# Differential attention's output, computed with the queries on the partitions, block by block

## The chip, the cores and the metric

The kernel runs on one core of a Trainium2 chip. The metric is device time in microseconds (us) for one execution. A core has a matrix engine (TensorE, PE in the profile, with its weight loads shown as PEld), a vector engine (VectorE, DVE), a scalar engine (ScalarE, ACT), a general one (GpSimd, POOL) and a queue engine (SyncE, SP) that starts transfers. Each engine works through its own instructions in the order in which they stand in its queue and waits on semaphores of the others.

## What is computed

Two transformer blocks, one after the other, on 512 tokens of width 1024. The change is in the second block's differential attention, eight heads of 128 value columns:

```python
# q, k: (B, S, H, 2, 64) after an RMS norm; v: (B, S, H, 128)
s = jnp.einsum("bhmqd,bhmkd->bhmqk", qblk, kt).astype(jnp.float32) * scale
s = s + bias[None, :, None]                    # distance bias of the head
s = jnp.where(dist >= 0, s, -jnp.inf)          # causal
p = jax.nn.softmax(s, axis=-1)
a = (p[:, :, 0] - lam * p[:, :, 1]).astype(vt.dtype)
o = jnp.einsum("bhqk,bhkd->bhqd", a, vt)
...
o = rms_norm_2(o, subln_g) * (1.0 - lambda_init)   # over the head's 128 columns
o = o.reshape(B, S, DIFF_WIDTH) * jax.nn.silu(gate)
return o @ w_proj
```

The block also has a convolution branch (31 taps over 1024 channels, then a layer norm), a cross-attention branch over 256 memory tokens, and a gated sum of the three branches.

## The kernel before, in words

All arithmetic is float32 in effect: an operand is split into a high part (a rounded copy, made by ACT) and a low part (the rest, made by DVE or POOL by a subtraction), and a product takes three matmuls, high by high, high by low, low by high. In the names, `hh`/`hl` are the normed input's two parts, `wh`/`wl` those of a weight block, `pth`/`ptl` those of the transposed attention weights, `dvh`/`dvl` those of the values.

The second block's attention stage runs from about 400 us to about 735 us of the span. `staged` walks over 32 items, eight heads `h` by four query blocks `n` of 128 queries. In step `i` it calls `diff_first` on item `i` (scores, mask and minimum on DVE, exponentials on ACT, then DVE divides and subtracts the two maps), `diff_pv` on item `i-2`, `diff_tp` on item `i-1` (PE transposes the attention weights, ACT and DVE split them), and then `fill`, which issues one to three pieces of other work: projections of the queries, keys, values and gates of later heads and of the other branches, 24 or 12 matmuls each, with their weight loads and splits. The instructions of an engine stand nearly in this order. An exception is the convolution (`cv`, L902 and L904, 31 DVE operations for each of eight channel groups), which has a low priority and is laid between other DVE work when the program is built; the order is fixed from then on.

The steps that the change touches, per head: `causal_tp` fills one pair of tiles `pth`/`ptl` over all four query blocks. At the head's last block, `diff_pv` multiplies them with the values, which are the stationary operand, so that the output lies with the value columns on the partitions and the 512 queries along the row (L1056, twelve matmuls of 512, 384, 256 and 128 columns, three each). ACT squares the output and copies it out of PSUM (L1059, L1060). In the next head's steps, `rsum` sums the squares over the partitions by a product with a column of ones (L225), ten small DVE operations make the reciprocal root (`rsqrt_small`), `rdiag` writes its four blocks as diagonal matrices (L234), `rbc` multiplies them with ones to spread them over the partitions (L240), and DVE scales the output by them and by the gain (L1070). `spill` multiplies by the gate (L933), splits (L934, L935) and stores both parts for the projection that comes later. PSUM tiles come from small pools: two for scores (`sc`), two for transposes and sums (`tp`), one for the attention output (`pv`), three for projections (`mm`).

Of the kernel before, what the change touches and what calls it, by code (L numbers as in the profile page):

```python
# [11 lines left out]
F32 = mybir.dt.float32  # L12
# [8 lines left out]
P = 128  # L21
S = 512
# [71 lines left out]
def two_block_kernel(ctx: ExitStack, tc: tile.TileContext, A: dict, out: bass.AP):  # L94
# [229 lines left out]
    with ExitStack() as st:  # L324
# [119 lines left out]
        after(dve.tensor_scalar(out=sub8, in0=V("subln"), scalar1=0.8, scalar2=None, op0=ALU.mult), first)  # L444
# [426 lines left out]
    with ExitStack() as st:  # L871
        wk = open_pool(st, "wk2", 2, reuse_waits="tile")
        dp = open_pool(st, "dp", 2, reuse_waits="tile")
        cm_[0] = open_pool(st, "cm2", 1, reuse_waits="tile")
# [88 lines left out]
        def dv_gen(g):  # L963
            w = w2("dv", g)
            vh = dp.tile([P, NT, CW], F32R, tag="dvh", name="dvh")
            vl = dp.tile([P, NT, CW], F32R, tag="dvl", name="dvl")
            for tp in range(2):
# [5 lines left out]
                pv_ = ps.rearrange("p (t d) -> p t d", t=2)  # L973
                d = slice(2 * tp, 2 * tp + 2)
                act.copy(out=vh[:, d, :], in_=pv_)
                dve.tensor_tensor(out=vl[:, d, :], in0=pv_, in1=f(vh[:, d, :]), op=ALU.subtract)
                yield
            D["dv", g] = (vh, vl)
# [56 lines left out]
        def diff_tp(it):  # L1035
            h, n = it
            causal_tp(it, D.pop(it), n, (n + 1) * P, ("dpt", h))

        def diff_pv(it):
            h, n = it  # L1040
            if n == 0 and h > 0:
                D["ss", h - 1] = rsum(D.pop(("oq", h - 1)))
            if n == 1 and h > 0:
                D["dg", h - 1] = rdiag(wk, D.pop(("ss", h - 1)), 1.0 / 128, 1e-6, "or")
            if n == 2 and h > 0:
                diff_out(h - 1)
            if n < NT - 1:
                return
            pth, ptl = fxd.pop(("dpt", h))
            vh, vl = D["dv", h // 2]  # L1050
            c0 = (h % 2) * P
            pv = pv_tile()
            for j in range(NT):
                a, b = vh[:, j, c0:c0 + P], vl[:, j, c0:c0 + P]
                for i, (l_, r_) in enumerate(((a, pth), (a, ptl), (b, pth))):
                    pe.matmul(out=pv[:, j * P:], lhsT=l_, rhs=r_[:, j, j * P:], start=(j == 0 and i == 0), stop=(j == NT - 1 and i == 2))  # L1056
            o = wk.tile([P, S], F32, tag="do", name="do", bufs=3)
# [4 lines left out]
            if h == 7:  # L1062
                D["ss", h] = rsum(q)
# [378 lines left out]
```

## Time and profile before

| | us |
|---|---|
| median of 3 runs | 1195.09 |
| lowest, highest | 1194.05, 1196.65 |
| profiled execution, its own time | 1196.61 |
| its span (first to last instruction) | 1194.8 |
| PE busy in the span | 1154.0 (97%) |
| DVE busy in the span | 926.6 (78%) |
| ACT busy in the span | 551.7 (46%) |
| POOL busy in the span | 213.3 (18%) |

A busy share is an average over stages, and a matmul's recorded duration includes time in which the next one has started already. What a matmul costs in a stream is the distance from its start to the start of the next.

### The profile page before, as it was taken

How to read it: one execution, taken by the hardware profiler on the slowest of the kernel's cores; microseconds unless marked ns; L12 is line 12 of the kernel's file. 1: busy time of each engine (PE TensorE's matmuls, PEld its weight loads, DVE VectorE, ACT ScalarE, POOL GpSimd, SP SyncE). 2: the span in 40 equal slices, each digit the busy share in tenths (PEclk: the TensorE clock that was granted, in tenths of full speed). 3: DMA queues.
4: the chain of work that ended last, by engine and by line, in shares of the span. 5: the costliest groups of instructions: out<-in, count | busy, mean ns of one | idle time of the engine just before them, and what ended most of it. 6: DMA issues, size and time to landing. Idle time of an engine off the chain costs nothing.

```text
span 1194.8 us, 18995 instructions
## 1 busy us (share of the span) xinstructions
PE 1154.0 (97%) x6960; PEld 1015.9 (85%) x6960; DVE 926.6 (78%) x2055; ACT 551.7 (46%) x1173; POOL 213.3 (18%) x161
## 2 busy tenths in 40 slices
PE   7879999999989999999999999999999999999998
PEld 6878887878889988998999887988888888888898
DVE  6997777898686699999989999999692596543341
ACT  7646566557554354445554452544422354232230
POOL 1334200000112211120111221221010132011020
PEclk9989999999999999999999999999999999999999
DMA  8765312443463423324233343333446755433232
GB/s 336 259 212 164 105 56 87 152 148 110 150 231 131 124 71 98 106 89 115 89 116 106 124 141 106 106 116 106 152 147 227 267 186 185 132 97 101 86 123 79
DMA packets 61965, 165.43 MB, mean 138 GB/s; under 512 B 7120, under 2 KB 15568, under 8 KB 60848
## 3 DMA queue, kind: packets, MB, share of 16 engines
q1 hardware_dynamic: 36560, 122.41, 32.5%
q10 hardware_dynamic: 25312, 41.82, 10.0%
q8 instruction: 55, 0.90, 0.3%
q14 instruction: 38, 0.31, 0.1%
HBM read 136.80 MB, written 20.58 MB: 132 GB/s over the span
## 4 chain that ended last, share of the span: by engine, by line
PE 63%; DVE 24%; issue 3%; ACT 1%; DMA 0%; POOL 0%; ACTq 0%; DVEq 0%; POOLq 0%
PE mm L190 40%; PE mm L199 15%; DVE cv L904 7%; DVE wl L171 3%; DVE dp L1025 1%; PE pv L773 1%; DVE dp L1032 1%; PE tp L751 1%; DVE dp L1031 1%; DVE ptl L754 1%; PE sc L1157 1%; PE pv L694 1%; PE pv L1200 1%; DVE qs L259 1%; PE tp L266 1%
## 5 line engine op out<-in xcount | busy, mean ns | idle before, releaser
L169 ACT CAST wh<-raw 128x512 fp32r<-128x512 f32 x372 | 215.3, 620 | 217.7 <-PE mm L190 96.2
L171 POOL TENSOR_TENSOR wl<-raw,wh 128x512 fp32r<-128x512 f32 (+1 forms) x93 | 141.8, 1525 | 831.9 <-ACT wh L169 668.8
L171 DVE TENSOR_TENSOR wl<-raw,wh 128x512 fp32r<-128x512 f32 (+1 forms) x279 | 201.7, 747 | 95.3 <-ACT wh L169 94.9
L190 PE MATMUL mm<-hh,wh 128*128 128x512 f32 x640 | 255.9, 400 | 0.0
L190 PE MATMUL mm<-hh,wl 128*128 128x512 f32 x640 | 251.8, 393 | 0.0
L190 PE MATMUL mm<-hl,wh 128*128 128x512 f32 x640 | 251.7, 393 | 0.0
L199 PE MATMUL mm<-wh,hh 128*128 128x256 f32 (+1 forms) x672 | 193.5, 289 | 0.2 <-ACT hh L824 0.2
L904 DVE SCALAR_TENSOR_TENSOR cv<-u,vec,cv 128x512 f32<-128x512 f32 x240 | 191.1, 796 | 3.4
L199 PE MATMUL mm<-wl,hh 128*128 128x256 f32 (+1 forms) x672 | 190.7, 284 | 0.3 <-POOL wl L171 0.3
L199 PE MATMUL mm<-wh,hl 128*128 128x256 f32 (+1 forms) x672 | 190.8, 284 | 0.0
L190 PEld LDWEIGHTS mm<-hh,wl 128*128 128x128 f32 x640 | 120.5, 188 | 27.0
L190 PEld LDWEIGHTS mm<-hh,wh 128*128 128x128 f32 x640 | 120.6, 188 | 24.7
L190 PEld LDWEIGHTS mm<-hl,wh 128*128 128x128 f32 x640 | 120.8, 189 | 24.5
L199 PEld LDWEIGHTS mm<-wl,hh 128*128 128x128 f32 x672 | 128.5, 191 | 0.8 <-POOL wl L171 0.6
L199 PEld LDWEIGHTS mm<-wh,hh 128*128 128x128 f32 x672 | 127.9, 191 | 0.8 <-ACT hh L824 0.5
L199 PEld LDWEIGHTS mm<-wh,hl 128*128 128x128 f32 x672 | 128.3, 191 | 0.0
L190 PE MATMUL mm<-bh,wh 128*128 128x512 f32 x192 | 75.9, 396 | 0.0
L190 PE MATMUL mm<-bh,wl 128*128 128x512 f32 x192 | 75.4, 393 | 0.0
L190 PE MATMUL mm<-bl,wh 128*128 128x512 f32 x192 | 75.4, 393 | 0.0
L1027 ACT ACTIVATE dp<-dp,dst 128x128 f32<-128x128 f32 (+3 forms) x64 | 35.5, 556 | 54.8 <-DVE dst L1025 54.6
L199 PE MATMUL mm<-wl,mh 128*128 128x256 f32 x128 | 39.3, 307 | 6.5 <-DVE wl L171 6.5
L190 PEld LDWEIGHTS mm<-bl,wh 128*128 128x128 f32 x192 | 36.1, 188 | 8.4 <-issue 0.2
(326 smaller groups left out, 2122.4 us busy)
## 6 DMA issues: line engine op xcount, KB each, us to landing
raw<-in_w_dram SPq DMA_DIRECT2D x120, 512.0 KB
raw<-in_w_out_dram SPq DMA_DIRECT2D x24, 512.0 KB
raw<-in_w_mem_dram SPq DMA_DIRECT2D x16, 512.0 KB
ada<-in_w_ada_dram SPq DMA_DIRECT2D x8, 1024.0 KB
ada<-in_w_gate_dram SPq DMA_DIRECT2D x8, 512.0 KB
k<-ks SPq DMA_DIRECT2D x32, 128.0 KB
o_d<-sph ACTq DMA_DIRECT2D x16, 256.0 KB
o_d<-spl ACTq DMA_DIRECT2D x16, 256.0 KB
```

Source lines behind the costliest of these rows:

```text
L169: act.copy(out=wh[:, s], in_=raw[:, s])
L171: eng.tensor_tensor(out=wl[:, s], in0=raw[:, s], in1=f(wh[:, s]), op=ALU.subtract)
L190: m = pe.matmul(out=ps, lhsT=a[:, c0:c0 + P], rhs=at(b, k), start=(n == 0 and i == 0), stop=(n == KT - 1 and i == 2))
L199: pe.matmul(out=ps, lhsT=at(a, k)[:, t * P:(t + 1) * P], rhs=b[:, 0:n], start=(start and m == 0 and i == 0), stop=(stop and m == len(order ...
L259: dve.scalar_tensor_tensor(out=s[b], in0=ps[a], scalar=sc, in1=f(s[a]), op0=ALU.mult, op1=ALU.subtract)
L266: pe.transpose(out=ps[:, t * P:(t + 1) * P], in_=src[:, t, c0:c0 + P], identity=ident)
L694: pe.matmul(out=pv4[0:64], lhsT=l_, rhs=r_[:, j], start=(cnt == 0), stop=(cnt == 3 * nk - 1))
L751: pe.transpose(out=tp[:, j * P:(j + 1) * P], in_=pt_[:, j * P:(j + 1) * P], identity=ident)
L754: dve.tensor_tensor(out=ptl[:, 0:n + 1, n * P:w], in0=tv, in1=f(pth[:, 0:n + 1, n * P:w]), op=ALU.subtract)
L773: pe.matmul(out=pv[0:64, j * P:], lhsT=l_, rhs=r_[:, j, j * P:], start=(j == 0 and i == 0), stop=(j == NT - 1 and i == 2))
L904: dve.scalar_tensor_tensor(out=a, in0=u[:, j:j + S], scalar=dw[:, m * 31 + j:m * 31 + j + 1], in1=a, op0=ALU.mult, op1=ALU.add)
L1027: act.activation(out=p_[:, :w], in_=p_[:, :w], func=AF.Exp, scale=-1.0, bias=st_[:, 0, n, m:m + 1], accum_out=st_[:, 1, n, m:m + 1])
```

## The change

The product is turned round. The attention weights of one query block are the stationary operand and the values stream past them: the high and low parts of the values lie side by side in one tile `dvv`, so that one matmul of 256 columns multiplies the high weights with both, and a second one of 128 columns multiplies the low weights with the high values. This is done for each block as it comes, for `n+1` key blocks. The queries are now on the partitions, so the sum of squares over a head's 128 columns runs along the row: ACT squares with an accumulator (`accum_out`). DVE adds the two halves of the PSUM tile. POOL multiplies the whole head by the reciprocal roots, PE transposes it (four transposes), and `spill` takes the gain, the gate and the factor a half in one DVE operation. `rsum`, `rdiag` and `rbc` are no longer called here. The tiles `pth`/`ptl` now hold one block and have two buffers.

```diff
-        after(dve.tensor_scalar(out=sub8, in0=V("subln"), scalar1=0.8, ...), first)
+        after(dve.tensor_scalar(out=sub8, in0=V("subln"), scalar1=0.4, ...), first)
...
-        cm_[0] = open_pool(st, "cm2", 1, reuse_waits="tile")
+        cm_[0] = open_pool(st, "cm2", 2, reuse_waits="tile")
...
-        def spill(o, z, hd_, ld_, i):
+        def spill(o, sc, z, hd_, ld_, i):
             a = wk.tile([P, S], F32R, tag="sph", name="sph", bufs=1)
             b = wk.tile([P, S], F32R, tag="spl", name="spl", bufs=1)
-            dve.scalar_tensor_tensor(out=o, in0=z, scalar=0.5, in1=o, op0=ALU.mult, op1=ALU.mult)
-            act.copy(out=a, in_=o)
-            dve.tensor_tensor(out=b, in0=o, in1=f(a), op=ALU.subtract)
+            dve.scalar_tensor_tensor(out=z, in0=o, scalar=sc, in1=z, op0=ALU.mult, op1=ALU.mult)
+            act.copy(out=a, in_=z)
+            dve.tensor_tensor(out=b, in0=z, in1=f(a), op=ALU.subtract)
...
-            vh = dp.tile([P, NT, CW], F32R, tag="dvh", name="dvh")
-            vl = dp.tile([P, NT, CW], F32R, tag="dvl", name="dvl")
+            vv = dp.tile([P, NT, 2, 2, P], F32R, tag="dvv", name="dvv")
...
         def diff_tp(it):
             h, n = it
-            causal_tp(it, D.pop(it), n, (n + 1) * P, ("dpt", h))
+            p_, w = D.pop(it), (n + 1) * P
+            pth = cm_[0].tile([P, NT, P], F32R, tag="pth", name="dpth")
+            ptl = cm_[0].tile([P, NT, P], F32R, tag="ptl", name="dptl")
+            tp = tp_tile()
+            for j in range(n + 1):
+                pe.transpose(out=tp[:, j * P:(j + 1) * P], in_=p_[:, j * P:(j + 1) * P], identity=ident)
+            tv = tp[:, :w].rearrange("p (j q) -> p j q", q=P)
+            act.copy(out=pth[:, 0:n + 1, :], in_=tv)
+            dve.tensor_tensor(out=ptl[:, 0:n + 1, :], in0=tv, in1=f(pth[:, 0:n + 1, :]), op=ALU.subtract)
+            D["dpt", h, n] = (pth, ptl)
 
         def diff_pv(it):
             h, n = it
             if n == 0 and h > 0:
-                D["ss", h - 1] = rsum(D.pop(("oq", h - 1)))
-            if n == 1 and h > 0:
-                D["dg", h - 1] = rdiag(wk, D.pop(("ss", h - 1)), 1.0 / 128, 1e-6, "or")
+                diff_norm(h - 1)
             if n == 2 and h > 0:
                 diff_out(h - 1)
-            if n < NT - 1:
-                return
-            pth, ptl = fxd.pop(("dpt", h))
-            vh, vl = D["dv", h // 2]
-            c0 = (h % 2) * P
+            pth, ptl = D.pop(("dpt", h, n))
+            vv = D["dv", h // 2]
+            if n == 0:
+                D["o", h] = (wk.tile([P, NT, P], F32, tag="do", name="do", bufs=3), wk.tile([P, NT], F32, tag="oss", name="oss"))
+            o, ss = D["o", h]
             pv = pv_tile()
-            for j in range(NT):
-                a, b = vh[:, j, c0:c0 + P], vl[:, j, c0:c0 + P]
-                for i, (l_, r_) in enumerate(((a, pth), (a, ptl), (b, pth))):
-                    pe.matmul(out=pv[:, j * P:], lhsT=l_, rhs=r_[:, j, j * P:], ...)
-            o = wk.tile([P, S], F32, tag="do", name="do", bufs=3)
-            q = wk.tile([P, S], F32, tag="doq", name="doq", bufs=1)
-            act.activation(out=q, in_=pv, func=AF.Square)
-            act.copy(out=o, in_=pv)
-            fill(1)
-            if h == 7:
-                D["ss", h] = rsum(q)
...
+            for j in range(n + 1):
+                v = vv[:, j, h % 2]
+                pe.matmul(out=pv[:, 0:256], lhsT=pth[:, j, :], rhs=v.rearrange("p a d -> p (a d)"), start=(j == 0), stop=False)
+                pe.matmul(out=pv[:, 0:P], lhsT=ptl[:, j, :], rhs=v[:, 0, :], start=False, stop=(j == n))
+            act.copy(out=o[:, n, :], in_=pv[:, P:256])
+            dve.tensor_tensor(out=o[:, n, :], in0=pv[:, 0:P], in1=o[:, n, :], op=ALU.add)
+            q = wk.tile([P, P], F32, tag="doq", name="doq", bufs=2)
+            act.activation(out=q, in_=o[:, n, :], func=AF.Square, accum_out=ss[:, n:n + 1])
+            if n == NT - 1:
+                fill(1)
+
+        def diff_norm(h):
+            o, ss = D["o", h]
+            r = rsqrt_small(wk, ss, NT, 1.0 / 128, 1e-6, "or")
+            pool.tensor_tensor(out=o, in0=o, in1=r.unsqueeze(2).to_broadcast([P, NT, P]), op=ALU.mult)
 
         def diff_out(h):
-            o = D.pop(("o", h))
-            r = rbc(D.pop(("dg", h)))
-            dve.scalar_tensor_tensor(out=o, in0=o, scalar=sub8, in1=r, op0=ALU.mult, op1=ALU.mult)
+            o, _ = D.pop(("o", h))
+            ps = transposed(o, 0)
             fill.until(("dg", h // 2))
-            spill(o, D["dg", h // 2, h % 2], odh_d, odl_d, h)
+            spill(ps, sub8, D["dg", h // 2, h % 2], odh_d, odl_d, h)
```

The two rows of cross-attention code that used `dvh` and `dvl` take halves of a `dvv` tile instead, and its `spill` calls pass 0.5.

The order of instructions moves at three places. First PE, before, at the second block of the third head's steps: `sc` are scores, `pv` the output of the head before, `mm` a projection of the fill.

```order
L1023 MATMUL sc<-klz_4539,qs 128x256
L1056 MATMUL pv<-pth,dvh 128x512
L1056 MATMUL pv<-ptl,dvh 128x512
L1056 MATMUL pv<-pth,dvl 128x512
L1056 MATMUL pv<-pth,dvh 128x384
L1056 MATMUL pv<-ptl,dvh 128x384
L1056 MATMUL pv<-pth,dvl 128x384
L1056 MATMUL pv<-pth,dvh 128x256
L1056 MATMUL pv<-ptl,dvh 128x256
L1056 MATMUL pv<-pth,dvl 128x256
L1056 MATMUL pv<-pth,dvh 128x128
L1056 MATMUL pv<-ptl,dvh 128x128
```

A whole head's output stood here in one run of twelve. Now PE at a head's first block: the four transposes of the head's scaled output `do` stand where `rbc` stood, and the output of one query block of the next head follows, in pairs.

```order
L1022 MATMUL sc<-klz_4543,qs 128x128
L266 MATMUL tp<-cst,do 128x128 x4
L1062 MATMUL pv<-dvv,dpth 128x256
L1063 MATMUL pv<-dvv,dptl 128x128
L1062 MATMUL pv<-dvv,dpth 128x256
L1063 MATMUL pv<-dvv,dptl 128x128
L1062 MATMUL pv<-dvv,dpth 128x256
L1063 MATMUL pv<-dvv,dptl 128x128
L1041 MATMUL tp<-cst,dp 128x128 x4
L190 MATMUL mm<-hh,wh 128x512
```

Every one of the 32 steps now has such pairs, one to four of them, and a `pv` tile of its own to be emptied before the next step's pairs. Third DVE, after, at a head's last block: the reciprocal of the row sums (L1028) waits for the exponentials, the new addition (L1065) for ACT's copy of half the `pv` tile, and L1044 is the low part of the transposed weights.

```order
L1024 ISA dp,dst<-sc,wb 128x512
L1024 ISA dst 128x1
L171 TENSOR_TENSOR wl<-raw,wh 128x512
L902 TENSOR_SCALAR cv<-u,vec 128x512
L904 SCALAR_TENSOR_TENSOR cv<-u,vec,cv 128x512
L1028 RECIPROCAL drr<-dst 128x2
L1065 TENSOR_TENSOR do<-pv,do 128x128
L1029 TENSOR_TENSOR drr<-drr,nlam 128x1
L1044 TENSOR_TENSOR dptl<-tp,dpth 128x384
L1030 TENSOR_SCALAR dp<-dp,drr 128x512
L904 SCALAR_TENSOR_TENSOR cv<-u,vec,cv 128x512
L1031 SCALAR_TENSOR_TENSOR dp<-dp,drr 128x512
```

An addition of this kind stands in all 32 steps, behind whatever part of the convolution was laid ahead of it; the number of `cv` operations up to each head is within four of what it was.

## Rows read from the trace of the kernel before

**Rows 1.** The page's first part: busy time of each engine.
```profile
PE 1154.0 (97%) x6960; PEld 1015.9 (85%) x6960; DVE 926.6 (78%) x2055; ACT 551.7 (46%) x1173; POOL 213.3 (18%) x161
```

**Rows 2.** Four stretches of 80 us: busy us of PE, PEld, DVE, ACT, POOL.
```profile
...
480.00:560.00 80.00, 77.45 (x541) 71.73 (x541) 78.14 (x185) 37.12 (x83) 12.19 (x8) 1.00 0.35 105
...
sum 320.00, PE 311.97 PEld 284.00 DVE 307.45 ACT 155.50 POOL 56.92; mean PE 77.99 PEld 71.00 DVE 76.86 ACT 38.87 POOL 14.23
```

**Rows 3.** Waits in 400 to 720 us: us in total, times, longest.
```profile
PE tp L266 <- DVE ptl L754: 2.9, 2, 1.6
...
PE tp L751 <- DVE rt L213: 1.2, 1, 1.2
...
DVE qs L259 <- ACT qs L258: 6.6, 2, 4.7
DVE dvl L976 <- ACT dvh L975: 2.0, 3, 0.9
DVE u L898 <- PE mm L190: 1.8, 3, 0.9
```

**Rows 4.** Timeline of PE at one head's output: start, duration, instruction.
```profile
602.70 0.40 PE L1056 MATMUL pv<-pth,dvh 128*128 128x512 f32 x1
602.94 0.40 PE L1056 MATMUL pv<-ptl,dvh 128*128 128x512 f32 x1
...
604.17 0.28 PE L1056 MATMUL pv<-pth,dvl 128*128 128x256 f32 x1
604.29 0.22 PE L1056 MATMUL pv<-pth,dvh 128*128 128x128 f32 x1
604.35 0.28 PE L1056 MATMUL pv<-ptl,dvh 128*128 128x128 f32 x1
604.46 0.27 PE L1056 MATMUL pv<-pth,dvl 128*128 128x128 f32 x1
604.57 0.34 PE L199 MATMUL mm<-wh,hh 128*128 128x256 f32 x1
604.74 0.28 PE L199 MATMUL mm<-wl,hh 128*128 128x256 f32 x1
```

**Rows 5.** The same view at a spreading product, a transposition and a sum of squares.
```profile
595.21 1.10 PE L240 MATMUL tp<-rdiag,cst 128*128 128x128 f32 x8
596.15 0.60 PE L751 MATMUL tp<-cst,dp 128*128 128x128 f32 x4
596.50 0.48 PE L190 MATMUL mm<-hh,wh 128*128 128x512 f32 x1
596.82 0.39 PE L190 MATMUL mm<-hl,wh 128*128 128x512 f32 x1
...
620.51 0.95 PE L225 MATMUL tp<-cst,doq 128*128 128x1 f32 x8
621.32 0.42 PE L751 MATMUL tp<-cst,dp 128*128 128x128 f32 x2
```

**Rows 6.** DVE's groups by form, 400 to 740 us: busy us, mean ns.
```profile
L904 DVE SCALAR_TENSOR_TENSOR cv<-u,vec,cv 128x512 f32<-128x512 f32 x147 | 115.7, 787 | 1.3
L234 DVE TENSOR_SCALAR rdiag<-cst,ry 128x128 f32<-128x128 f32 x32 | 8.6, 310 | 0.1
L1070 DVE SCALAR_TENSOR_TENSOR do<-do,sub,tp 128x512 f32<-128x512 f32 x8 | 5.9, 738 | 0.2 <-PE tp L240 0.2
L754 DVE TENSOR_TENSOR ptl<-tp,pth 128x128 fp32r<-128x128 f32 x8 | 2.3, 282 | 0.0
```

**Rows 7.** ACT's groups by form, 400 to 720 us.
```profile
L753 ACT CAST pth<-tp 128x128 fp32r<-128x128 f32 x8 | 2.1, 269 | 6.6 <-PE tp L751 4.9 <-DVE u L897 1.7
...
L1027 ACT ACTIVATION_READ_ACCUMULATOR dp<-dp,dst 128x1 f32 x64 | 12.0, 187 | 0.0
```

**Rows 8.** Timeline of DVE and of POOL around one POOL multiplication.
```profile
522.35 1.99 DVE L1032 SCALAR_TENSOR_TENSOR dp<-dp,drr 128x128 f32<-128x128 f32 x1
...
521.70 2.49 POOL L961 TENSOR_TENSOR qn<-qn,ry 128x1024 f32<-128x1024 f32 x1 [6.99 <-DVE ry L219]
```

More of the change, by code (lines that the diff above doesn't have):

```diff
@@ L443, in two_block_kernel @@
         after(dve.tensor_scalar(out=V("dw"), in0=V("dw"), scalar1=0.5, scalar2=None, op0=ALU.mult), first)
-        after(dve.tensor_scalar(out=sub8, in0=V("subln"), scalar1=0.8, scalar2=None, op0=ALU.mult), first)
+        after(dve.tensor_scalar(out=sub8, in0=V("subln"), scalar1=0.4, scalar2=None, op0=ALU.mult), first)
         lt = pa1.tile([P, 2, 64], F32, name="lt")
@@ L972, in dv_gen @@
                         yield
-                pv_ = ps.rearrange("p (t d) -> p t d", t=2)
+                pv_ = ps.rearrange("p (t h d) -> p t h d", t=2, h=2)
                 d = slice(2 * tp, 2 * tp + 2)
-                act.copy(out=vh[:, d, :], in_=pv_)
-                dve.tensor_tensor(out=vl[:, d, :], in0=pv_, in1=f(vh[:, d, :]), op=ALU.subtract)
+                act.copy(out=vv[:, d, :, 0, :], in_=pv_)
+                dve.tensor_tensor(out=vv[:, d, :, 1, :], in0=pv_, in1=f(vv[:, d, :, 0, :]), op=ALU.subtract)
                 yield
-            D["dv", g] = (vh, vl)
+            D["dv", g] = vv
         def dqk_gen(g):
@@ L1053, in diff_pv @@
-            for j in range(NT):
-                a, b = vh[:, j, c0:c0 + P], vl[:, j, c0:c0 + P]
-                for i, (l_, r_) in enumerate(((a, pth), (a, ptl), (b, pth))):
-                    pe.matmul(out=pv[:, j * P:], lhsT=l_, rhs=r_[:, j, j * P:], start=(j == 0 and i == 0), stop=(j == NT - 1 and i == 2))
-            o = wk.tile([P, S], F32, tag="do", name="do", bufs=3)
-            q = wk.tile([P, S], F32, tag="doq", name="doq", bufs=1)
-            act.activation(out=q, in_=pv, func=AF.Square)
@@ L1060, in diff_pv @@
-            act.copy(out=o, in_=pv)
-            fill(1)
-            if h == 7:
-                D["ss", h] = rsum(q)
-            D["oq", h] = q
-            D["o", h] = o
+            pth, ptl = D.pop(("dpt", h, n))
[3 more added lines that the diff above has]
+            o, ss = D["o", h]
+            pv = pv_tile()
+            for j in range(n + 1):
+                v = vv[:, j, h % 2]
+                pe.matmul(out=pv[:, 0:256], lhsT=pth[:, j, :], rhs=v.rearrange("p a d -> p (a d)"), start=(j == 0), stop=False)
+                pe.matmul(out=pv[:, 0:P], lhsT=ptl[:, j, :], rhs=v[:, 0, :], start=False, stop=(j == n))
@@ L1067, in diff_out @@
         def diff_out(h):
-            o = D.pop(("o", h))
-            r = rbc(D.pop(("dg", h)))
-            dve.scalar_tensor_tensor(out=o, in0=o, scalar=sub8, in1=r, op0=ALU.mult, op1=ALU.mult)
+            o, _ = D.pop(("o", h))
+            ps = transposed(o, 0)
             fill.until(("dg", h // 2))
-            spill(o, D["dg", h // 2, h % 2], odh_d, odl_d, h)
-            D["done", h] = True
+            spill(ps, sub8, D["dg", h // 2, h % 2], odh_d, odl_d, h)
         def dgate_gen(g):
@@ L1125, in two_block_kernel @@
         staged([(h, n) for h in range(8) for n in range(NT)], diff_first, diff_tp, diff_pv, 1, lambda i: 2 + (i % 3 == 0) - (i < 28 and i % 4 == (2 if i // 4 % 2 else 0)))
-        D["dg", 7] = rdiag(wk, D.pop(("ss", 7)), 1.0 / 128, 1e-6, "or")
+        diff_norm(7)
         fill(1)
@@ L1132, in cross_pro @@
             qn = D["xq", hd]
-            qh = dp.tile([P, 2, S], F32R, tag="dvh", name="xqh")
-            ql = dp.tile([P, 2, S], F32R, tag="dvl", name="xql")
+            qhl = dp.tile([P, 2, 2, S], F32R, tag="dvv", name="xqh")
+            qh, ql = qhl[:, 0], qhl[:, 1]
             for k in range(2):
@@ L1207, in cross_pv @@
             for i in range(2):
-                spill(os_[i], D["xg", hd][i], oxh_d, oxl_d, 2 * hd + i)
+                spill(os_[i], 0.5, D["xg", hd][i], oxh_d, oxl_d, 2 * hd + i)
             if hd < 2:
```

## The prediction

> **What bounds the kernel now.** I read the page's first part first: PE is busy 97% of the span, DVE 78% [rows 1]. For the whole kernel that says PE. The change lies in one stage, so the second view is the busy time by stretch from 400 to 720 us, which is that stage but for its first and last few us. There PE is busy 311.97 of 320 us and DVE 307.45, while ACT has 155.50 and POOL 56.92; in the stretch from 480 to 560 DVE has 78.14 of 80, more than PE [rows 2]. Two engines are full at once. The third view, the waits, says which of them waits: PE loses 8 us (320 less 311.97), most of it in the transposes and products that need a `tp` tile, until DVE has read an older one; DVE loses 12.6 us (320 less 307.45), 10.4 of it in three waits for ACT and PE [rows 2, 3]. So the stage runs at PE's pace with DVE close behind it, and DVE's 31-step convolution work is what fills it. A saving on PE counts up to the point at which DVE can't follow. Both engines have to be costed.
>
> **PE, per head.** In a stream of matmuls the cost is the distance between starts.
>
> Removed: the twelve matmuls of the output, from 602.70 to 604.57, are 1.87 us; the projection's first matmul behind them takes 0.17 (604.57 to 604.74) where its like takes 0.12 (the 256-column matmul at 604.17), so the last narrow matmul costs its successor 0.05 more, in all 1.92 [rows 4]. The sum of squares takes 0.81 (620.51 to 621.32) and the spreading product 0.94 (595.21 to 596.15); each is four products in the code and eight matmuls in the trace [rows 5]. Together 3.67 us.
>
> Added: ten pairs, a matmul of 256 columns and one of 128. The trace has both kinds, but no such alternation. A 256-column matmul takes 0.12 behind another one and 0.17 behind a 128-column one; a 128-column matmul takes 0.06 behind a 256-column one and 0.11 behind its like [rows 4]. Alternating, that is 0.17 + 0.06 = 0.23 us a pair; counted as if each stood among its like it is 0.12 + 0.11, again 0.23. I take 0.23, so 2.30 for ten pairs. The lowest that these rows allow is 0.12 + 0.06 = 0.18, in which narrow matmuls hide wholly (1.80), the highest 0.17 + 0.11 = 0.28 (2.80). Twenty weights are loaded where twelve were; their cost is in these distances. The four transposes of the scaled output are like those at 596.15: 0.35, and 0.09 more for the matmul behind them, which takes 0.32 (596.50 to 596.82) where one of 512 columns takes 0.23 or 0.24 in a stream (602.70 to 602.94) [rows 4, 5]: 0.44 in all.
>
> So 3.67 less 2.74 is 0.93 us a head, **7.4 us for eight heads**. With the pair at 0.18 it would be 11.4, at 0.28 it would be 3.4.
>
> The two kinds of 128-column cost show that half the columns don't bring half the price: 0.11 against 0.12 between matmuls of one kind [rows 4]. The Trainium skill ("TensorE: Matmul & The Clock Gate", section "Back-to-back issue gap") gives about 81 ns for a matmul of 128 columns in a stream of weight loads and matmuls. By it the ten narrow matmuls would be 0.81 and the saving some 2.3 us larger, an estimate from that page; the trace doesn't agree with it, and 0.11 is used.
>
> **DVE, per head.** Removed: four diagonal blocks at 310 ns and the scaling at 738 ns, 1.98 us. Added: four additions of 128 columns out of PSUM, priced like the 128-column split that also reads PSUM, 282 ns, 1.13 us. `spill`'s product now reads PSUM, and I price it like the old scaling, 0.74 against 0.68, 0.06 more. Net 0.79 less [rows 6], 6.3 us over eight heads. The ten small operations of the root stay, one step earlier.
>
> **POOL against DVE.** The new multiplication of 512 columns a head has its nearest row in the one of 1024 columns: 2.49 us, so about 1.2. While that one ran, DVE's 128-column operation with two operands in SBUF took 1.99 us; the 128-column split costs 0.28 [rows 6, 8]. So an operation of DVE stands still until POOL is done. Most of what DVE does there, the convolution above all, has two such operands. What a new multiplication takes from DVE lies between nothing (DVE happens to read PSUM) and 1.2 us; with the convolution at about a third of DVE's time (115.7 us [rows 6]) and the divides beside it I take half, 0.6, so 5 us in eight heads, bounds 0 and 9.6. DVE's work is then 6.3 less and 5 more: nearly what it was, while PE's is 7.4 less.
>
> **ACT.** It loses two passes of 512 columns a head and gets four copies and four squares of 128 columns, with an accumulator read each: 269 ns a pass and 187 for the read [rows 7], so about 8 × 0.27 + 4 × 0.19 = 2.9 us a head for some 1.2. ACT is busy half the stage [rows 2], so the time itself is covered. What is not covered is its order: ACT's copy waits for PE, DVE's addition for the copy, ACT's square for the addition, and behind the square stand a split of transposed weights and casts of the next weight block. DVE's addition has the divides of the attention weights queued behind it, for which PE's transposes of the next step wait.
>
> **The sum.** PE gives 7.4 us. DVE sets how much of it can be had. It has about 306 us of work in the stretch (307.45 - 6.3 + 5) and 10.4 us of waits for ACT and PE that the change leaves alone [rows 2, 3]; if all of them stay it needs 316.6 of the 320, and the gain is 3.4. New handovers to ACT come on top: if one addition in four waits for a copy of 0.27 us, 8 × 0.27 = 2.2, and the gain is about 1.2. On the other side PE no longer waits for the `tp` tile that held the sums of squares (1.2 us, the row of `rt` [rows 3]). Between 1.2 and 7.4 + 1.2 I take **4.5 us**, near the middle, since neither engine alone sets the pace. Transfers, the weights' order and the later stages are the same. The profiled execution, 1196.61 us, would come to 1192.1. It stands 1.5 above the median of the runs, 1195.09, so the median after is 1190.6. A change of 0.2% (2.4 us) is about what a measurement of this kernel can tell from none.
>
> **Rivals.**
> 1. The whole gain of PE and more: narrow matmuls hide behind the wide ones (0.18 a pair) and the `tp` waits go. 11.4 us less gives 1183.7, 8 us less 1187. For it speaks the 0.06 behind a wide matmul; against it the 0.17 that the next wide one then takes [rows 4].
> 2. DVE becomes the bound and nothing is gained. If each POOL multiplication stops it for the full 1.2 us, its work is 307.45 - 6.3 + 9.6 = 310.8, and with the 10.4 us of waits 321: the stage takes as long as before, 1195 to 1196. For it speaks the stretch with 78.14 of 80 us [rows 2]; against it, that part of its waits only shows that it is ahead. The Trainium skill ("SBUF — State Buffer", section "Who interferes with whom") says that VectorE and GpSimd share a port pair, that a VectorE instruction with two SBUF inputs contends with GpSimd reads, and that the loser blocks for the whole instruction. The trace agrees: 1.99 us under a POOL operation [rows 8].
> 3. Slower, by the single `pv` tile. It is now filled in every step and must be emptied by ACT's copy and DVE's addition before the next step's pairs; before, a head had it for four steps. PE stands in order, so a late addition holds scores, transposes and projections. The gain is eaten when it costs 7.4 / 32 = 0.23 us a step. If the addition stands one convolution operation (0.787 us [rows 6]) too late in half of the steps, 16 × 0.787 = 12.6, the kernel is 5.2 us slower: 1200.3. Against it: the same step's transposes wait for a DVE result that stands behind the addition in DVE's queue, and PE waits for such results little today [rows 3].
>
> **Chances.** Forecast (1.2 to 8.6 us less, its own range 1187 to 1194) 0.55, of which one part in six lies within 2.4 us; rival 1 beyond that 0.10; rival 2 0.18; rival 3 0.17. Faster by over 0.2% is 0.46 + 0.10 = 0.56, plus a little of rival 2 where DVE's waits are half slack, 0.60. Within 0.2%: 0.25. Slower: 0.15, nearly all rival 3. The range of 1185.5 to 1198.5 leaves out the far part of rival 1 and the greater part of rival 3, together under 0.2.
>
> **What would show it.** In the profile after: pairs at 0.23 us between starts, no L225 or L240 in this stage, PE's instructions there some 7 us shorter; DVE's addition near 0.28 us and its waits for ACT longer by 1 to 3 us; DVE operations of over 1 us under the new POOL multiplication; PE's waits in 400 to 720 us between 8 and 12. Pairs under 0.2 would make rival 1 right; DVE busy at 99% with PE waits over 15 us rival 2; waits of the first matmul of a pair for the addition (PE on `pv`), 0.2 us or more a step, rival 3. The forecast is wrong above all if the fixed order of DVE puts an addition or a root behind convolution work that PE needs sooner.

## The result and the profile after

The changed kernel takes 1204.78 us in the median of six runs (1198.86 to 1206.96), the kernel before 1195.47 beside it. The ratio is 1.0072, with a 95% interval of 1.0051 to 1.0093: **slower by about 9 us**, where 4.5 us faster was forecast, and outside the range of 1185.5 to 1198.5. The profiled execution took 1204.16 us, 7.6 more than the one before.

The page's first part, after, against [rows 1]:

```profile
PE 1147.0 (95%) x6928; PEld 1008.5 (84%) x6928; DVE 927.2 (77%) x2047; ACT 560.7 (47%) x1253; POOL 222.2 (18%) x169
```

PE's busy time fell by 7.0 us, near the 7.4 of the forecast, and the kernel became longer all the same. The busy time by stretch from 400 to 720 us, against [rows 2] (same columns):

```profile
480.00:560.00 80.00, 73.61 (x517) 68.38 (x516) 77.49 (x182) 39.28 (x103) 14.71 (x9) 1.00 0.34 99
...
sum 320.00, PE 303.30 PEld 277.11 DVE 304.83 ACT 159.90 POOL 61.89; mean PE 75.82 PEld 69.28 DVE 76.21 ACT 39.98 POOL 15.47
```

PE is now busy less than DVE. To see where the time went, I put a window on each kernel from the first scores of head 0 to the first scores of the cross-attention (busy us of PE, PEld, DVE, ACT, POOL). Before:

```profile
410.60:733.10 322.50, 314.47 (x2054) 285.38 (x2053) 312.74 (x748) 153.22 (x343) 57.35 (x34) 1.00 0.35 107
```

After:

```profile
410.10:738.80 328.70, 310.61 (x2026) 282.01 (x2025) 315.84 (x741) 161.73 (x423) 64.80 (x42) 0.99 0.34 103
```

The stage is 6.2 us longer. DVE's share of it is much the same (97.0%, then 96.1%), PE's falls from 97.5 to 94.5%. On DVE's account the 6.2 us are 3.1 of work and 3.1 of idle time (9.8 to 12.9); on PE's they are 3.9 less work and 10.1 more idle time. Such an account closes for every engine, so it doesn't say which of them sets the pace; the experiments have to. Where DVE's idle time grew is seen in its waits (400 to 720 us, to compare with [rows 3]):

```profile
DVE qs L259 <- ACT qs L258: 4.9, 2, 4.7
DVE u L898 <- PE mm L190: 3.4, 4, 1.0
DVE drr L1028 <- ACT dp L1026: 3.1, 5, 0.9
```

The wait of the reciprocal (L1028) for ACT's exponentials is new. PE's waits in the same stretch, the six longest:

```profile
PE tp L1041 <- DVE dp L1031: 5.7, 4, 3.6
PE tp L266 <- DVE rt L218: 2.5, 1, 2.5
PE pv L1063 <- DVE dptl L1044: 2.3, 2, 1.3
PE tp L266 <- DVE qs L259: 1.8, 3, 1.0
PE pv L1062 <- DVE cv L904: 1.2, 1, 1.2
PE tp L1041 <- ACT do L1064: 0.9, 1, 0.9
```

With four rows of 0.4 to 0.6 us they come to 16.4 us, where the kernel before had 7.9. All but one are waits for DVE.

For a finer measure I take the distance from each matmul's start to the next one's in this window, and count as work what such a matmul takes in a stream (0.23 us for 512 columns, 0.12 for 256 and so on, by [rows 4, 5]), and as loss what goes beyond, waits and a lower clock alike. Before, the 322.5 us are an estimated 312.0 of work and 10.5 of loss; after, 328.7 are 304.2 and 24.6. **PE's work fell by 7.8 us, and its loss grew by 14.1.** Behind the stage the changed kernel loses another 1.9 us. PE's wait for DVE at the start of the cross-attention is longer there, first before, then after:

```profile
PE tp L240 <- DVE xql L1138: 2.5, 1, 2.5
...
PE tp L266 <- DVE xqh L1145: 3.8, 1, 3.8
```

### The profile page after: what moved, and what is told of

The parts are those of the page before. It is cut to its first block, busy times and chain, and to the rows that moved or that the text cites. A ratio compares the mean times of both kernels' runs of the same rounds, so it can differ in the third digit from the quotient of the medians.

```text
span 1202.4 us, 19037 instructions
## 1 busy us (share of the span) xinstructions
PE 1147.0 (95%) x6928; PEld 1008.5 (84%) x6928; DVE 927.2 (77%) x2047; ACT 560.7 (47%) x1253; POOL 222.2 (18%) x169
## 4 chain that ended last, share of the span: by engine, by line
PE 62%; DVE 30%; issue 3%; ACT 2%; DMA 2%; POOL 0%; ACTq 0%; SPq 0%; DVEq 0%; POOLq 0%
PE mm L190 39%; PE mm L199 16%; DVE cv L904 8%; DVE wl L171 5%; DVE acc L319 2%; DVE dp L1024 1%; DVE dp L1031 1%; DVE qs L259 1%; PE sc L1164 1%; DMA raw<-in_w_out_dram 1%; PE pv L694 1%; PE pv L773 1%; DVE dp L1030 1%; PE pv L1207 1%; DVE ss L957 1%
## 5 line engine op out<-in xcount | busy, mean ns | idle before, releaser
L171 DVE TENSOR_TENSOR wl<-raw,wh 128x512 fp32r<-128x512 f32 (+1 forms) x279 | 200.8, 745 | 107.4 <-ACT wh L169 106.9
L171 POOL TENSOR_TENSOR wl<-raw,wh 128x512 fp32r<-128x512 f32 (+1 forms) x93 | 138.7, 1492 | 768.0 <-ACT wh L169 675.2
```

The lines of the kernel that those rows point to most:

```text
L171: eng.tensor_tensor(out=wl[:, s], in0=raw[:, s], in1=f(wh[:, s]), op=ALU.subtract)
```

## How the largest wait comes about

PE's timeline in the seventh head (start, duration, instruction, and in brackets the idle time before it):

```profile
664.25 0.28 PE L1062 MATMUL pv<-dvv,dpth 128*128 128x256 f32 x1
664.37 0.22 PE L1063 MATMUL pv<-dvv,dptl 128*128 128x128 f32 x1
664.42 0.34 PE L1062 MATMUL pv<-dvv,dpth 128*128 128x256 f32 x1
664.60 0.22 PE L1063 MATMUL pv<-dvv,dptl 128*128 128x128 f32 x1
668.43 0.90 PE L1041 MATMUL tp<-cst,dp 128*128 128x128 f32 x3 [3.61 <-DVE dp L1031]
```

The wide matmul behind a narrow one takes 0.18 us (664.42 to 664.60), the narrow one behind it 0.05 (664.37 to 664.42): a pair is 0.23 us, as forecast. Then PE stands for 3.61 us until DVE has divided the attention weights of this block. DVE's timeline shows where they were:

```profile
661.56 0.89 DVE L218 TENSOR_TENSOR rt<-rt,ru 128x4 f32<-128x4 f32 x1
...
662.98 1.47 DVE L171 TENSOR_TENSOR wl<-raw,wh 128x512 fp32r<-128x512 f32 x1
664.38 0.15 DVE L1028 RECIPROCAL drr<-dst 128x2 f32<-128x2 f32 x1
664.45 0.67 DVE L171 TENSOR_TENSOR wl<-raw,wh 128x512 fp32r<-128x512 f32 x1
665.04 1.21 DVE L1029 TENSOR_TENSOR drr<-drr,nlam 128x1 f32<-128x1 f32 x1
666.18 0.74 DVE L904 SCALAR_TENSOR_TENSOR cv<-u,vec,cv 128x512 f32<-128x512 f32 x1
666.84 0.41 DVE L1030 TENSOR_SCALAR dp<-dp,drr 128x384 f32<-128x384 f32 x1
667.17 0.67 DVE L248 SCALAR_TENSOR_TENSOR zg<-gt,mm 128x512 f32<-128x512 f32 x1
667.77 0.60 DVE L1031 SCALAR_TENSOR_TENSOR dp<-dp,drr 128x384 f32<-128x384 f32 x1
```

and POOL's beside it:

```profile
660.02 2.41 POOL L961 TENSOR_TENSOR xqn<-xqn,ry 128x1024 f32<-128x1024 f32 x1 [6.76 <-DVE ru L217]
662.87 1.04 POOL L1074 TENSOR_TENSOR do<-do,ry 128x512 f32<-128x512 f32 x1 [0.43 <-DVE ry L219]
664.73 1.51 POOL L171 TENSOR_TENSOR wl<-raw,wh 128x512 fp32r<-128x512 f32 x1 [0.82 <-ACT wh L169]
```

DVE has no gap here. A root's operation on four columns takes 0.89 us under POOL's norm, a split of 0.67 takes 1.47 under the new multiplication (L1074), a one-column product takes 1.21 under a split of POOL's. Between the links of the chain that PE waits for (L1028, L1029, L1030, L1031) stand a split, a convolution step and a gate, as the build laid them. From start to start these three take 1.9 us, and POOL's stop of the one-column product about 1 us more. So the order of DVE's instructions and POOL's stops have a part in this wait; the same load in another order was not tried. The kernel before waits at the same step, the seventh head's third block, for less:

```profile
663.59 0.52 PE L751 MATMUL tp<-cst,dp 128*128 128x128 f32 x3 [1.15 <-DVE rt L213]
```

PE's pause after the change costs something more (windows, with the granted clock as the third number from the end):

```profile
664.00:668.40 4.40, 0.82 (x6) 0.60 (x4) 4.40 (x9) 0.60 (x2) 1.51 (x1) 0.91 0.70 211
668.40:674.50 6.10, 6.07 (x16) 4.92 (x17) 6.07 (x13) 3.10 (x9) 1.58 (x2) 0.50 0.35 108
674.50:680.00 5.50, 5.50 (x27) 4.54 (x26) 5.46 (x8) 2.22 (x6) 0.99 (x1) 1.00 0.33 95
```

Behind the pause the granted clock is 0.50, the 1.2 GHz level, for 6.1 us, in which PE is busy throughout; its 512-column matmuls start 0.43 us apart and not 0.23. That is some 3 us, in the 24.6 above.

## The experiments

Theory A: DVE sets the pace of this stage, so PE's saving can be had only as far as DVE has room, and each further stop or handover of DVE lengthens it. Rival B: the loss lies in the new steps' own handovers, whatever DVE's load (in the form B1, in ACT's squares standing ahead of what PE waits for). Rival C, formed on the way: DVE's freed time fills up with convolution, so that relief of DVE brings nothing. In the expectations of experiments 1, 3 and 5 the letter C still stands for something else, that the pairs cost PE more than 0.23 us; the 0.23 above speaks against that. The changed kernel's ratio of 1.0072 is what each ratio below is held against, unless it says otherwise; 0.001 is 1.2 us.

**1. scale_on_act** and **no_scale**: the multiplication by POOL.

```diff
-            pool.tensor_tensor(out=o, in0=o, in1=r.unsqueeze(2).to_broadcast([P, NT, P]), op=ALU.mult)
+            for n in range(NT):
+                act.activation(out=o[:, n, :], in_=o[:, n, :], func=AF.Copy, scale=r[:, n:n + 1])
```

> The changed kernel with the multiplication by the reciprocal roots on ACT (four passes of 128 columns a head with a scale per partition) in the place of POOL's one of 512 columns. Theory A (DVE is the bound of the stage and every POOL multiplication stops it, some 5 us in eight heads): 4 to 7 us less than the changed kernel's 1204.8, so 1198 to 1201, and DVE operations of over 1 us under the new POOL work are gone. Theory B (the bound is the chain of handovers in each step, ACT's copy, DVE's addition, ACT's square, whatever DVE's load): no gain, 1204 to 1207, since ACT has some 1.2 us a head more to do. Theory C (PE itself: the alternating matmuls cost more than 0.23 us a pair): no change.

Measured: 1203.49 us, ratio 1.0076 (1.0062 to 1.0090). Nothing gained: A's 4 to 7 us did not come, and no gain is what B had expected. Later I took the POOL line away with nothing in its place.

> The changed kernel without POOL's multiplication of the output by the reciprocal roots (left out: that scaling of the heads' outputs; the roots are still worked out). DVE loses about 5.2 us under the eight multiplications, and the transposes of the output no longer wait for POOL. In the kernel before, seven such multiplications cost 6 us. Theory A (each stop of DVE comes out as a PE wait, since DVE has no room): 4 to 7 us gained, 1198 to 1201. If the freed time goes to convolution work, as with the other reliefs of DVE: 0 to 3 us, 1202 to 1205.

Measured: 1199.16, ratio 1.0033 (1.0023 to 1.0044), 5 us gained, as A has it. So the eight POOL multiplications cost some 0.6 us each, and four ACT passes in their place cost as much again. But where the gain lies fits A only in part. In the profiled execution the stage is 1.9 us shorter, and 5.3 us are gained behind it, where PE's wait for `xqh` (3.8 us after, 0.8 here) and the low clock that follows it are gone. The window from 738 to 760 us, of the changed kernel and then of no_scale:

```profile
738.00:760.00 22.00, 18.19 (x99) 15.78 (x97) 17.18 (x29) 8.12 (x19) 3.89 (x3) 0.84 0.43 132
...
738.00:760.00 22.00, 21.21 (x146) 19.34 (x146) 19.25 (x33) 9.49 (x22) 3.04 (x2) 1.00 0.39 131
```

PE's waits under scale_on_act contain one that the kernel otherwise hardly has, for ACT:

```profile
PE pv L1063 <- DVE dptl L1044: 4.9, 4, 1.4
...
PE pv L1062 <- ACT dpth L1043: 2.1, 2, 1.9
```

That ACT's passes delay the split of the transposed weights fits this row; it was not tested by itself.

**2. before_plus_pool**: the kernel before with a POOL multiplication by ones in each of seven heads.

```diff
             if n == 1 and h > 0:
                 D["dg", h - 1] = rdiag(wk, D.pop(("ss", h - 1)), 1.0 / 128, 1e-6, "or")
+                x = D["o", h - 1]
+                pool.tensor_tensor(out=x, in0=x, in1=ones[:, 0:1].to_broadcast([P, S]), op=ALU.mult)
             if n == 2 and h > 0:
```

> The kernel before with one more multiplication of 512 columns on POOL for each of the first seven heads (by one, so that nothing changes in the values), at the step where the roots are made. It prices POOL's work alone. If what it takes from DVE (some 0.7 us each in the trace of the changed kernel) reaches the end, 1199 to 1201; if DVE makes it up in the gaps behind each convolution group, 1195 to 1197.

Measured: 1201.11, ratio 1.0058 (1.0042 to 1.0074). Such a multiplication costs the old kernel 0.9 us, on an engine that is busy 18%. Neither PE nor DVE waits for POOL's result in this stage. Part of the price is TensorE's clock: the granted clock is 0.98 in each of the two stretches from 400 to 560 us, where it was 1.00.

**3. three_narrow**: no DVE addition; three matmuls of 128 columns into the same columns.

```diff
-                pe.matmul(out=pv[:, 0:256], lhsT=pth[:, j, :], rhs=v.rearrange("p a d -> p (a d)"), ...)
+                pe.matmul(out=pv[:, 0:P], lhsT=pth[:, j, :], rhs=v[:, 0, :], ...)
+                pe.matmul(out=pv[:, 0:P], lhsT=pth[:, j, :], rhs=v[:, 1, :], ...)
...
-            act.copy(out=o[:, n, :], in_=pv[:, P:256])
-            dve.tensor_tensor(out=o[:, n, :], in0=pv[:, 0:P], in1=o[:, n, :], op=ALU.add)
+            act.copy(out=o[:, n, :], in_=pv[:, 0:P])
```

> The changed kernel with three matmuls of 128 columns a key block, all into the same 128 columns, so that ACT copies the finished sum and DVE's 32 additions are gone (8.9 us of DVE). PE pays some 0.1 us more a key block, 8 us in all. Theory A: DVE's relief and PE's cost nearly cancel against the changed kernel, with DVE the bound the sum is a gain of 0 to 6 us, 1199 to 1205. Theory B: the chain loses one handover in 32 steps, a gain of 5 us or more, under 1200. Theory C: 8 us slower, 1212 or more.

Measured: 1216.0, ratio 1.0179 (1.0165 to 1.0192). PE's work is 8.7 us more by the measure above (312.9), and the loss 31.3, although DVE has 32 operations less. Of the loss 7.2 us are one wait for ACT at the end of the window:

```profile
PE sc L1164 <- ACT xqh L1144: 7.2, 1, 7.2
```

A had 1199 to 1205 and missed by 11 us. If DVE alone set the pace, 8.9 us less of its work should not have left the rest of the loss where it was (24.1 us, against 24.6). The time lies where the C of these first expectations had it (1212 or more), but pairs of 0.23 us speak against that one too. This run is not explained.

**4. late_square**: the squares moved from each step into `diff_norm`.

> The changed kernel with ACT's four squares of a head not in the steps but together, two steps later, just before the reciprocal roots. ACT then never waits for DVE's addition with the split of the transposed weights queued behind it. Theory B1 (the square, waiting for the addition, holds up ACT's high part, so DVE's low part and PE's output matmuls; in the trace 5.9 us of waits at output matmuls and 18 us of ACT waiting for additions): 3 to 6 us less than the changed kernel's 1204.8, so 1199 to 1202. Theory A (DVE is late because the convolution work laid into its queue leaves it no room): under 2 us, 1203 to 1205, with the waits moved to other instructions.

Measured: 1207.48, ratio 1.0105 (1.0092 to 1.0118), slower. The stage is as long as without the edit, so B1 falls.

**5. DVE's load.** In both kernels the convolution is cut short (left out: 15 of 30 steps in each of eight groups, or, with `range(1, 24)`, 7 of 30).

```diff
-                for j in range(1, 31):
+                for j in range(1, 16):
```

> The kernel before with 15 of the 30 accumulating convolution steps of each channel group left out (the convolution then has 16 taps of 31), which takes some 95 us of work off DVE, most of it in the attention stage. It is the partner of the next run. All theories: PE waits less in the stage; 1182 to 1193.

> The changed kernel with the same 15 convolution steps left out. Theory A: DVE can follow, and the change shows PE's saving, 5 to 9 us less than the kernel before with the same cut. Theory B: the handovers cost what they did, so it is still slower than its partner by 4 us or more. Theory C: also still slower, with the loss on PE between the pairs.

> The kernel before with 23 convolution steps after the first in each group instead of 30 (left out: the last seven taps of the convolution). Half of the taps (15) gained 7.4 us. Theory A: 2 to 5 us gained, 1190 to 1193.

> The changed kernel with the same cut (the last seven taps left out). Half of the taps gained 23.6 us here. Theory A: the greater part of it comes with the first seven, 10 to 17 us gained, 1188 to 1195, within 3 us of before_taps_23 on either side: with full convolution the changed kernel is 9.3 us slower, with half 6.5 faster. If the loss belonged to the steps and not to DVE's load: at least 5 us slower than before_taps_23.

| convolution steps | before | changed | changed less before |
|---|---|---|---|
| 30 | 1195.47 (1) | 1204.78 (1.0072) | +9.3 |
| 23 | 1192.13 (0.9969) | 1194.47 (0.9993) | +2.3 |
| 15 | 1187.69 (0.9939) | 1181.18 (0.9887) | −6.5 |

The difference passes through zero, as A demands; a loss in the steps themselves, whatever DVE's load (B), would stay. In the profiled executions the stage itself says the same: it is 6.2 us longer than before with 30 steps, 0.9 longer with 23 and 6.1 shorter with 15. What the cut can't tell apart is DVE's load and its order, since it also takes convolution steps from between the results that PE waits for. With half of the steps the sum of the stretches from 400 to 720 us is, before:

```profile
sum 320.00, PE 315.54 PEld 288.20 DVE 275.43 ACT 155.86 POOL 54.88; mean PE 78.88 PEld 72.05 DVE 68.86 ACT 38.97 POOL 13.72
```

and changed, with PE's longest wait:

```profile
sum 320.00, PE 314.86 PEld 287.48 DVE 271.52 ACT 166.26 POOL 59.86; mean PE 78.71 PEld 71.87 DVE 67.88 ACT 41.56 POOL 14.97
...
PE pv L1063 <- DVE dptl L1044: 2.7, 2, 1.4
```

With DVE at 85 to 86% PE is full in both, and the loss is an estimated 5.5 and 7.2 us. Then 6.5 us of PE's saving are in the time.

**6. conv_later**: in both kernels the order of the fill starts the convolution's later groups later, which takes 31 steps out of this stage.

```diff
-    "dqk0 dv0 glu0 dqk1 dg0 dv1 glu1 dqk2 dg1 dv2 glu2 dqk3 dg2 dv3 glu3 xq0 dg3 xg0 xq1 glu4 m11 glu5 m12 glu6 m13 glu7 m20 m21 m22 m23"
+    "dqk0 dv0 glu0 dqk1 dg0 dv1 m11 dqk2 dg1 dv2 glu1 dqk3 dg2 dv3 glu2 xq0 dg3 xg0 xq1 glu3 m12 glu4 m13 glu5 m20 glu6 m21 glu7 m22 m23"
```

> The changed kernel with another order of the fill: one convolution group fewer lies in the attention stage (a merge gate takes its place), and the groups behind it come one place later, so that 31 convolution steps, 24 us of DVE, move out of the stage to where DVE has room. Nothing is left out. Theory A: PE's waits in the stage fall by 8 us or more, 1192 to 1198. Theory B1: no change in the stage's waits but at places that happen to fall under the moved group, 1201 to 1206.

> The kernel before with the same other order of the fill, the partner of the run above. Theory A: it waits little today, so it gains 0 to 5 us, 1190 to 1196, and is then no faster than the changed kernel with this order. Theory B1: 1193 to 1197, still ahead of its partner by 5 us or more.

Measured: changed 1198.29, ratio 1.0026 (1.0014 to 1.0039), 6 us gained; before 1204.04, 1.0077 (1.0065 to 1.0089), 9 us lost. The latter's attention stage is 4.3 us shorter, but the layer norm behind the convolution is then late:

```profile
PE tp L1248 <- DVE lns L1245: 9.3, 1, 9.3
```

So the times of the pair can't be compared. The stage can (first before, then changed):

```profile
409.50:727.70 318.20, 313.31 (x2055) 285.24 (x2053) 290.23 (x713) 154.18 (x344) 56.30 (x34) 1.00 0.36 108
...
409.30:734.00 324.70, 311.83 (x2027) 283.50 (x2025) 294.53 (x710) 162.68 (x424) 61.89 (x42) 0.98 0.35 106
```

The changed kernel's is still 6.5 us longer, as B had it. Both are relieved mainly in the stretch from 480 to 560 us, and there PE is full in both (79.51 and 79.48 of 80). In the two stretches behind it, PE has 79.03 and 78.81 before, 75.67 and 73.95 changed, with DVE at 74 to 79 in all four. So the loss goes where DVE is given room and stays where it isn't, but a full DVE alone doesn't make it: the old steps run beside one without it.

**7. Lambda folded** into the pass that scales the second map, which takes 32 DVE operations (L1029 after, 297 ns) out of the stage:

```diff
-            dve.tensor_tensor(out=rr[:, n, 1:2], in0=rr[:, n, 1:2], in1=nlam, op=ALU.mult)
-            dve.tensor_scalar(out=pms[1][:, :w], in0=pms[1][:, :w], scalar1=rr[:, n, 1:2], scalar2=None, op0=ALU.mult)
+            dve.tensor_scalar(out=pms[1][:, :w], in0=pms[1][:, :w], scalar1=rr[:, n, 1:2], scalar2=nlam, op0=ALU.mult, op1=ALU.mult)
```

> The changed kernel with the factor lambda taken in the pass that already scales the second map (a second scalar of that DVE operation), so that the small DVE multiplication of the second reciprocal in each step is gone: 32 operations of 0.297 us, 9.5 us of DVE's 316 in the stage, 0.3 us in each step's chain, and nothing of PE, ACT or POOL. Theory A (DVE sets the pace in this stage, the PE saving is there but is had only as far as DVE has room): PE's waits in the stage go from 24.6 us to about 17, the kernel comes to 1196 to 1200, a gain of 5 to 9 us, and at least 2 us more than the same edit gives the kernel before. Theory C (freed DVE time is filled with convolution at once, so that waits stay what they were): under 3 us gained. Theory B (the loss lies in handovers of the new steps that don't depend on DVE's load): as much gained as in the kernel before, within 1 us.

> The same edit in the kernel before: 9.5 us of DVE less in the stage, PE's work unchanged. Its PE waits there are 10.5 us, of which half went when half of the convolution was left out. Theory A: 2 to 5 us gained, 1190 to 1193, less than the changed kernel gains. Theory C: under 2 us. Theory B: the same gain as in the changed kernel, within 1 us.

> The changed kernel with lambda folded as above and also POOL's multiplication of the output replaced by four ACT passes, so that DVE isn't stopped under POOL in the heads (another 5 us). Theory A: 2 to 5 us below fold_lambda_after, since DVE's room is no longer the whole limit: 1192 to 1197. Theory C, and a version of A in which ACT's four passes stand in front of the splits that PE waits for: no lower than fold_lambda_after, within 1.5 us, as it was without the fold.

> The changed kernel without POOL's multiplication (left out, as in no_scale) and with lambda folded. DVE is relieved of 5.2 and 9.5 us. Alone they gave 5.6 and 4.9 us. Theory A (DVE's load): they add up as long as waits are left, 1193 to 1196, at the kernel before or just below it. If the two remove the same waits: 1197 to 1199.

| | median | ratio, 95% interval |
|---|---|---|
| fold_lambda_after | 1199.88 | 1.0038 (1.0024 to 1.0052) |
| fold_lambda_before | 1197.74 | 1.0019 (1.0009 to 1.0029) |
| fold_scale_on_act | 1201.97 | 1.0050 (1.0035 to 1.0065) |
| no_scale_fold | 1195.11 | 0.9994 (0.9983 to 1.0006) |

In the changed kernel the edit gains 0.0034 (4 us, where A had 5 to 9); in the one before it gains nothing, and even loses 2 us, against the expectation: by the profile the stage is as long as without it (322.6 us), so what DVE is given there was not what the old kernel lacked; the 2 us are lost behind the stage and not followed further. Scaling on ACT is no help again. The two reliefs add up: 0.0039 and 0.0034 alone, 0.0078 together. C, which had under 3 us, falls for the changed kernel.

**8. pv_after_fill**: the output's product behind the step's other work, in effect:

```diff
                 diff_first(its[i])
-            if i >= 2: diff_pv(its[i - 2])
             if 0 <= i - 1 < 32: diff_tp(its[i - 1])
             fill(...)
+            if i >= 2: diff_pv(its[i - 2])
```

> The changed kernel with the output's product of a block behind the step's pieces of other work instead of in front of its transposes; nothing is added or left out. The pairs of a step then have some 6 us more until they need the split (dptl, DVE), for which PE waits 4 to 5 us in the stage now. If that wait is a loss of its own: 2 to 5 us gained, 1200 to 1203. If DVE's load is the bound and a wait that is taken away comes back at the next result: under 1.5 us either way, 1203.5 to 1206. If it's better that the pairs stand early, since the root of the head's last block is later now: slower, above 1206.

Measured: 1202.49, ratio 1.0058 (1.0043 to 1.0073), at most 2 us gained. PE's waits from 400 to 740 us:

```profile
PE tp L1041 <- DVE dp L1031: 14.4, 12, 4.4
PE tp L1041 <- DVE qs L259: 2.7, 3, 1.2
PE tp L1041 <- DVE klz L1002: 1.0, 1, 1.0
PE pv L1062 <- DVE do L1065: 0.5, 1, 0.5
```

The waits for `dptl` are gone, and those for `dp` went from 5.7 to 14.4; the loss in the stage is 25.3 us where it was 24.6. The time lies in the range of "a loss of its own" (1200 to 1203); the waits say the other thing: the one that is taken away comes back at the next result of DVE. The run does not decide between them.

**9. Versions.** fold_conv_later_after has edits 6 and 7; pv_after_fill_mix has edits 6, 7 and 8.

> The changed kernel with lambda folded and the order of the fill in which the convolution's second group starts later (31 convolution steps fewer in the stage, as in conv_later_after, 1198.3 us). Theory A: the two reliefs add up, 4 to 8 us below conv_later_after: 1190 to 1194, below the kernel before. Theory C: 1197 to 1199, as without the fold. What may spoil it for both: the layer norm of the convolution waits for the late groups, as it did in the kernel before with this order (9.3 us).

> The changed kernel, whole, with the output's product behind the fill, lambda folded and the convolution's second group later. fold_conv_later_after, without the first edit, took 1193.2. If pv_after_fill gains alone, 2 to 4 us less, 1189 to 1191; otherwise within 1.5 us of 1193.

Measured: 1193.19, ratio 0.9980 (0.9969 to 0.9992), and 1194.77, ratio 0.9992 (0.9981 to 1.0002). The first is the fastest whole kernel here, 0.2% below the kernel before. Its stretch from 480 to 560 us:

```profile
480.00:560.00 80.00, 79.39 (x573) 74.60 (x572) 59.73 (x148) 43.68 (x110) 14.39 (x10) 1.00 0.38 116
```

Where DVE is given room (59.73 of 80), PE is full with the new steps. Later in the stage DVE is fuller again (78.17 of 80 from 560 to 640 us), and the version gains less than PE's 7 us. The kernel before has a stage that is 4.3 us shorter with this order of the fill too (experiment 6), so the gain in the stage isn't the change's alone.

## Why the prediction was wrong, step by step

- **What bounds the kernel.** "So the stage runs at PE's pace with DVE close behind it" is half right. Without the change PE does wait little. But DVE had no room either: the seven POOL operations of experiment 2 cost the old kernel over 6 us. Room alone was not what it lacked, as 9.5 us less of DVE's work brought it nothing (experiment 7).
- **PE, per head: right.** Pairs at 0.23 us, no L225 or L240 in the stage, 7.8 us less work where 7.4 was forecast. By the Trainium skill's 81 ns for 128 columns ("TensorE: Matmul & The Clock Gate", "Back-to-back issue gap") the saving would have been some 2.3 us larger, an estimate from that page. The pairs of 0.23 us don't agree with it.
- **DVE and POOL: prices nearly right, total off.** The groups after (columns as in [rows 6]), POOL's new multiplication first, then three of DVE's:

```profile
L1074 POOL TENSOR_TENSOR do<-do,ry 128x512 f32<-128x512 f32 x8 | 10.5, 1308 | 57.8 <-DVE ry L219 30.1 <-ACT wh L169 18.1 <-ACT qs L258 9.5
...
L904 DVE SCALAR_TENSOR_TENSOR cv<-u,vec,cv 128x512 f32<-128x512 f32 x143 | 115.0, 804 | 1.3
L1065 DVE TENSOR_TENSOR do<-pv,do 128x128 f32<-128x128 f32 x32 | 8.9, 278 | 0.0
L933 DVE SCALAR_TENSOR_TENSOR zg<-tp,sub,zg 128x512 f32<-128x512 f32 x7 | 5.2, 742 | 0.0
```

  POOL's 1.2 us measured 1.31, the addition's 282 ns 278, `spill`'s 0.74 us 0.742. Added up, DVE's busy time in the stage should have fallen by 1.3 us (6.3 less, 5 more), and it grew by 3.1. The eight stops under POOL came to about 5.2 us (expectation of no_scale), as forecast. The 6.3 was too much, since it takes whole durations, which overlap a little: by the groups' busy time, the diagonal blocks and the scaling are 8.6 and 5.9 [rows 6], the addition is 8.9 and `spill` 0.5 more, so 5.1 less. The other 3 us lie in work that the change doesn't touch. The convolution steps rose from 787 to 804 ns in the mean, and the splits (L171) and the one-column product lengthened too; which POOL operations did that was not worked out. What the Trainium skill ("SBUF — State Buffer", "Who interferes with whom") says of the loser, that it blocks for the whole instruction, agrees with the timeline above: DVE's one-column product, started at 665.04 under POOL's split (664.73 to 666.24), ends at 666.25.
- **ACT: right in kind.** DVE's new waits for ACT are 3.1 us where 2.2 was forecast; they stand at the reciprocal, not at the addition.
- **The sum: this step failed.** I took 4.5 us, "near the middle, since neither engine alone sets the pace". Such a middle supposes that a late DVE can only take a share of PE's saving. The runs showed that it can take more: PE's work fell by 7.8 us, and its waits and low clock grew by 14.1. Experiment 5 shows that this loss depends on DVE's convolution load, and that the saving comes out (6.5 us) when half of that load is gone. Two terms of the sum were mistaken as well. It held DVE's 316.6 us against the 320 of the stretch, but the same sum for the kernel before is 317.85 (307.45 + 10.4); so the terms gave DVE 1.3 us and not 3.4, and with 2.2 us of new handovers nothing. And the wait of 1.2 us that should go (the row of `rt`) is the one at 663.59: at that step the changed kernel waits 3.61.
- **Rival 2** named the engine and not the size: it had no change as its end. Its mark, PE waits over 15 us, came true (16.4); "busy at 99%" did not (96%).
- **Rival 3** got the sign and not the place. PE waited on the `pv` tile's addition or what stands ahead of it once, for 1.2 us, and not 0.2 us a step. The last sentence of the prediction came nearest: convolution work stood in front of results that PE needed sooner, though these were the divides and not the addition.
- What stays open: whether DVE's total or the order of its instructions makes PE wait, as every cut of load also changed the order; why three_narrow lost so much; and how the remaining loss without POOL's multiplication (3.8 us by no_scale) divides among the chain's places in each step. Nor was it tried to let DVE add both halves from PSUM, without ACT's copy.

## What to carry to other kernels

Where two engines are both over 95% busy in a stage, work out the change for each of them alone, its work and its waits, and don't take the middle: here the saving on one became waiting for the other, and more. A small operation on an idle engine isn't free if it stops a full one: measure it by adding it to the old kernel. And to learn whether a loss lies in the change or in the load, take load from both kernels and see whether the difference changes its sign. Take it away over the whole stage; moved out of one stretch only, as in experiment 6, it leaves the rest as it was.

## What the hardware showed that was not expected

- A pause of 3.61 us on PE, behind a full stretch, was followed by 6.1 us at the 1.2 GHz level, though PE was busy all the time in them. In the kernel before, the longest wait within this stage is 1.6 us ([rows 3]) and the granted clock stays at 1.00. So this wait cost nearly twice its length.
- A POOL operation of 1.3 us delays the end of the kernel by 0.6 to 0.9 us, waits and low clock behind them included, with POOL idle for four fifths of the time.
- A short DVE operation can be held up as long as a large one: a one-column product took 1.21 us under POOL's split, where the mean of its 32 is 0.30.
